# Second and first blocks of late operands: loaded by GpSimd's DMA queue in place of SyncE's

## The chip, the cores and the metric

The kernel runs on one core of one Trainium2 chip. The metric is the device time of one execution in microseconds (us), the median of several runs. The engines are named as in the profile: PE (TensorE), PEld (TensorE's weight loads), DVE (VectorE), ACT (ScalarE), POOL (GpSimd) and SP (SyncE, which here only issues DMAs). A "q" behind an engine's name means its sequencer, which waits and issues.

## The reference

One layer of a hybrid decoder, batch 1, 512 tokens, width 2048, all in float32:

```
h    = rmsnorm(x)
u, v, q, k, v_att, g_a, g_b = split(h @ w_in)              # 1024 columns each, the gates 2048
y_a  = gelu(u) * (tril(w_s) applied per chunk of 128 to rmsnorm(gelu(v)) + b_s)
y_b  = stick_breaking_attention(rmsnorm(q), rmsnorm(k), v_att)   # 8 heads, strictly causal
x   += (sigmoid(g_a) * (y_a @ w_up_a) + sigmoid(g_b) * (y_b @ w_up_b)) @ w_o
x   += (silu(gate) * up) @ w_ffn_out      where gate, up = split(rmsnorm(x) @ w_ffn_in)   # 5632 wide
x   += sigmoid(rmsnorm(x) @ w_ple_gate) * (p @ w_ple)
```

## The kernel before

Everything is held transposed: an operand is a row of blocks of 256 features by 512 tokens, each block 128 partitions by 1024 float32, or 512 KB. A product of two float32 numbers is made of three matmuls of parts (high by high, high by low, low by high): ACT rounds a value to its high part, DVE subtracts to get the low one. The tiles `whi` and `wlo` hold those parts of the weights, the arena `parts` those of the operand, and the arena `wholes` holds everything that is not yet split: weights as they land, blocks as they are loaded, results.

A block of weights by a block of the operand is either "plain" (kind P, four quarter products, lines 296 to 298) or "S" (seven products of sums of quarters in place of eight, line 692). S needs seven blocks of each side where P needs four, and the sums are made on the fly:

- **Weights** (class `Weights`). A weight unit of kind S has two landing loads on SP's queue (line 341: one quarter into two places; line 343: the other three quarters). Then POOL issues an accumulating DMA (`landed`, line 363) that adds two more quarters onto the doubled one. It can go only when line 341's load has landed. ACT then makes the high parts (line 359), DVE two more sums (line 375), and DVE the low parts (line 356). Four landing buffers and three slots of `whi`/`wlo` go round. A unit of kind P has one load on SP's queue (line 339) and no accumulating DMA.
- **Late operands** (`late_form` with `plain_first`). Where an operand of the next stage is only just finished, its block is first loaded and split as four plain quarters (lines 286, 287, or 541, 542 with a gain), and PE starts in kind P. The same block is then loaded a second time (`fetch_second`), DVE makes the sums of quarters (line 527, behind line 522 on ACT where there is a gain), they are split in their turn, and PE goes on in kind S. The first and the second load of such a block are the "first and second ones" of this change. Blocks of kind P (`plain_form`) have a first load alone.

The operands that go through HBM are `mix` (the merged branches, 8 blocks, for `w_o`), `x1` (8 blocks, for `w_ffn_in`), `hid` (22 blocks, for `w_ffn_out`, which is worked off in three passes of 8, 8 and 6 blocks) and `x2` (8 blocks, for the last gate). SP stores each block when it is made (lines 1344, 1386, 1405, 1442); `spilled_form` gives its loads. In the trace and in the order `x1` and `x2` are both `x`, and a load is line 518 whatever it reads. Other loads of line 518 are of `xT`, of the gates, of `ple` and, as residuals, of `x`.

The order of the work: PE's matmuls stand in program order; `tick()` puts between them, one step a time, what prepares the next stage (fetching a block, splitting it, fetching a second one). A scheduler then sets the order of each engine's instructions from the dependencies. On each engine, and on each DMA queue's issuing engine, instructions go in order: one that waits holds back those behind it. POOL's own work in these stages is the accumulating DMAs of weights, those of results into `x1` (line 1438), and one small power for each norm (line 974).

Of the kernel before, what the change touches and what calls it, by code (L numbers as in the profile page):

```python
# [70 lines left out]
def hybrid_layer(  # L71
# [18 lines left out]
    nc = tc.nc  # L90
# [9 lines left out]
    def nm(s):  # L100
        return f"{s}_{next(names)}"
# [14 lines left out]
    class Arena:  # L116
# [5 lines left out]
        def take(self, n, how="low"):  # L122


            spots = []
            for start, size in self.holes:
                end = start + size
                if how == "place":
                    start = -(-start // (2 * PLACE)) * 2 * PLACE
                if end - start >= n:  # L130
                    if how == "high":
                        spots.append((-end, end - n))
                    elif how != "old":
                        spots.append((start, start))
                    else:
                        spots.extend((self.given[a // P : -(-(a + n) // P)].max(), a)
                                     for a in {*range(start, end - n + 1, 256), end - n})
            at = min(spots)[1]
            start, size = next(h for h in self.holes if h[0] <= at < h[0] + h[1])
            self.holes.remove((start, size))  # L140
            self.holes.extend(
                h for h in ((start, at - start), (at + n, start + size - at - n)) if h[1])
            return Block(self, at, n)
# [369 lines left out]
    def cut(x):  # L513
        return x.rearrange("p (b c) -> p b c", c=256)

    def load(src, n=1024, how="old"):
        b = take(n, how)
        nc.sync.dma_start(out=b.f(0, 1024), in_=src)
        return b

    def gained(dst, src, gi, k):
# [770 lines left out]
    def y_form(c, i):  # L1292
        return plain_form((lambda: y_a[i]) if c == "a" else lambda: load(y_spill[i]),
                          lambda: len(y_done) == 8, raw=0 if c == "a" else 1024,
                          far=c == "b")
# [3 lines left out]
    for n, ((w, i), pr) in enumerate(zip(order, made())):  # L1299
# [25 lines left out]
        else:  # L1325
# [8 lines left out]
    spill = {(n, j): tc.dram_tile([P, 1024], F32, name=nm(n)) for n in ("mix", "x1", "x2")  # L1334
             for j in range(KU)}
    there = set()

    def spilled_form(kind, n, j, gain=None, **how):
        return (late_form if kind == "S" else plain_form)(
            lambda size=1024: load(spill[n, j], size), lambda: (n, j) in there, gain, far=True,  # L1340
            **how)

    def store(n, j, block):
        nc.sync.dma_start(out=spill[n, j], in_=block.f())
        there.add((n, j))
        give(block)

    ms = [spilled_form("S", "mix", j) for j in range(KU)]
    build(ms)
    for j in range(KU):  # L1350
        for b in "ba":
            s = load(gate_spill[b, j], 1024, "low")
            g = s.f()

            def gate(g=g):
                scaled(g, row1)
                nc.scalar.activation(g, g, AF.Sigmoid)

            after(1, gate)
            pr = pair([ys[b, i] for i in range(4)], last=j == KU - 1)  # L1360
            for h, ps in zip((g[:, :T], g[:, T:]), pr.ends()):
                nc.vector.tensor_tensor(out=h, in0=h, in1=ps, op=ALU.mult)
            if b == "b":
                part[j] = s
            else:
                nc.vector.tensor_tensor(out=g, in0=g, in1=part[j].f(), op=ALU.add)
                give(part.pop(j))
                after(1, lambda j=j, s=s: store("mix", j, s))
        if not j:
            ple_operands()  # L1370
        elif j < 6:
            ple_pair(j + 2)
            if j == 5:
                ple_done()
    give(norm1.block)


    norm2 = Norm()
    fs = [spilled_form("S", "x1", j, (g_ffn, j)) for j in range(KU)]
    for j in range(KU):  # L1380
        h = load(xT[j])
# [14 lines left out]
    for kinds in PASSES:  # L1396
        hs.append([spilled_form(k, "hid", u)
                   for u, k in enumerate(kinds, sum(map(len, hs)))])
# [25 lines left out]
    for c, units in enumerate(hs):  # L1424
# [3 lines left out]
        for j in range(KU):  # L1428
# [8 lines left out]
            if not end:  # L1437
                after(2, lambda o=o, j=j: nc.gpsimd.dma_start(
                    out=spill["x1", j], in_=o, accum_op=ALU.add))
# [134 lines left out]
```

## Time and profile before

| | |
|---|---|
| median of 3 runs | 2661.22 us (2660.4 to 2664.61) |
| profiled execution | 2659.74 us, of which its span, first to last instruction, 2658.0 us |
| granted TensorE clock | 0.999 |
| busy: PE, PEld, DVE, ACT, POOL | 99%, 87%, 84%, 53%, 17% |
| SP's DMA queue | 441.95 MB in 231136 packets, 50.7% of 16 DMA engines' span |
| POOL's DMA queue | 115.11 MB in 62112 packets, 27.5% |

The stages by time from the span's start: projections and branches to about 840 us, `w_up` to 1036, `w_o` to about 1160, `w_ffn_in` to about 2040, `w_ffn_out` in three passes to about 2190, 2345 and 2485, the gate to the end.

A row of a timeline reads: start, duration, engine, line, operation, what it writes and reads, count, and in brackets how long its engine was idle before it and what ended that. A row of waits reads: who waited for what, microseconds in total, times, the longest. A row of DMA issues ends with KB each and the median microseconds from issue to landing. A row of windows reads: the stretch, its length, busy microseconds and number of instructions of PE, PEld, DVE, ACT and POOL, granted clock, the DMA engines' busy share, GB/s.

### The profile page before, as it was taken

What the parts mean: (1) busy time and instruction counts of PE and PEld (TensorE: products, weight loads), DVE (VectorE), ACT (ScalarE), POOL (GpSimd) and SP (SyncE); (2) the same over time, 40 slices, a digit from 0 to 9 for tenths busy, and PEclk for the clock granted to TensorE, in tenths of its full rate; (3) what the DMA queues carried; (4) which work ended last, traced back from release to release, by engine and by line L of the source; (5) the groups of instructions that cost most, each with busy time, mean ns of one, the idle gap of its engine ahead of it and who ended that gap; (6) DMA issues with size and microseconds to landing.
All of it is one profiled execution on the core that took longest, in us unless ns stands there. A gap on an engine that the chain in (4) does not pass through costs nothing.

```text
span 2658.0 us, 42554 instructions
## 1 busy us (share of the span) xinstructions
PE 2638.2 (99%) x15336; PEld 2312.3 (87%) x15336; DVE 2234.6 (84%) x3821; ACT 1403.2 (53%) x2233; POOL 448.1 (17%) x556
## 2 busy tenths in 40 slices
PE   8999999999999999999999999999999999999999
PEld 7888888888998888888888888888888888889898
DVE  8687878787886558999888888888889989989876
ACT  7756565655554334566444444444445445455543
POOL 0122222232220001101111111111110211211110
PEclk9999999999999999999999999999999999999999
DMA  7677777777775668978888888788887989978884
GB/s 229 162 194 171 192 173 191 172 191 179 178 191 183 232 212 268 265 236 218 223 210 216 206 200 203 194 209 204 199 207 221 257 227 273 229 229 260 256 240 123
DMA packets 293459, 559.77 MB, mean 211 GB/s; under 512 B 26368, under 2 KB 140544, under 8 KB 293248
## 3 DMA queue, kind: packets, MB, share of 16 engines
q1 hardware_dynamic: 231136, 441.95, 50.7%
q0 software_dynamic: 62112, 115.11, 27.5%
q8 instruction: 120, 1.97, 0.3%
q14 instruction: 91, 0.75, 0.1%
HBM read 505.57 MB, written 51.38 MB: 210 GB/s over the span
## 4 chain that ended last, share of the span: by engine, by line
PE 90%; DVE 4%; DMA 3%; issue 1%; ACT 1%; SPq 0%; POOL 0%; ACTq 0%; POOLq 0%; DVEq 0%
PE ps L692 53%; PE ps L298 10%; PE ps L297 9%; PE ps L296 9%; PE small L692 6%; DVE wlo L356 1%; DVE wholes L527 1%; DMA wholes<-w_ffn_out 1%; PE small L1103 1%; PE small L1155 1%; DVE parts L287 1%; PE small L1029 1%; DMA x<-wholes 1%; ACT whi L359 0%; PE small L1214 0%
## 5 line engine op out<-in xcount | busy, mean ns | idle before, releaser
L692 PE MATMUL ps<-parts,whi 128*128 128x512 f32 x4200 | 1409.4, 398 | 1.6 <-DVE out L796 1.0
L359 ACT ACTIVATE whi<-wholes 128x512 fp32r<-128x512 f32 (+2 forms) x940 | 871.5, 941 | 745.8 <-DVE wholes L375 286.6
L356 DVE TENSOR_TENSOR wlo<-wholes,whi 128x512 fp32r<-128x512 f32 (+2 forms) x940 | 979.4, 1076 | 73.7 <-ACT whi L359 73.0
L692 PEld LDWEIGHTS ps<-parts,wlo 128*128 128x128 f32 x4200 | 790.2, 188 | 178.2 <-issue 1.9
L692 PE MATMUL ps<-parts,wlo 128*128 128x256 f32 x4200 | 831.3, 279 | 0.9 <-DVE wlo L356 0.9
L692 PEld LDWEIGHTS ps<-parts,whi 128*128 128x128 f32 x4200 | 677.1, 189 | 10.5 <-issue 3.6
L297 PE MATMUL ps<-parts,whi 128*128 128x256 f32 (+1 forms) x1832 | 605.0, 331 | 0.7 <-DVE parts L287 0.5
L298 PE MATMUL ps<-parts,wlo 128*128 128x256 f32 (+1 forms) x1832 | 604.9, 331 | 0.5 <-DVE wlo L356 0.5
L296 PE MATMUL ps<-parts,whi 128*128 128x256 f32 (+1 forms) x1816 | 597.3, 330 | 7.4 <-ACT parts L286 5.3
L297 PEld LDWEIGHTS ps<-parts,whi 128*128 128x128 f32 x1832 | 347.0, 189 | 39.0 <-DVE parts L287 2.7
L296 PEld LDWEIGHTS ps<-parts,whi 128*128 128x128 f32 x1816 | 343.6, 190 | 40.4 <-ACT parts L286 5.7
L298 PEld LDWEIGHTS ps<-parts,wlo 128*128 128x128 f32 x1832 | 347.3, 190 | 32.4 <-DVE wlo L356 1.6
L375 DVE TENSOR_TENSOR wholes<-wholes 128x256 f32<-128x256 f32 (+1 forms) x820 | 345.0, 421 | 17.9 <-DVE wlo L356 1.4
L751 DVE TENSOR_TENSOR out<-out,ps 128x256 f32<-128x256 f32 x490 | 202.3, 416 | 147.6 <-ACT out L748 147.4
L363 POOL DMA_DIRECT2D wholes<-w_ffn_in x169 | 147.1, 870 | 702.1 <-DVE wholes L375 251.7
L363 POOL DMA_DIRECT2D wholes<-w_in x132 | 116.6, 885 | 531.3 <-DVE wholes L375 132.8
L692 PE MATMUL small<-parts,whi 128*128 128x512 f32 x480 | 190.3, 397 | 0.0
L287 DVE TENSOR_TENSOR parts<-wholes,parts 128x1024 fp32r<-128x1024 f32 (+3 forms) x137 | 122.8, 907 | 18.5 <-ACT parts L286 18.5
L286 ACT ACTIVATE parts<-wholes 128x1024 fp32r<-128x1024 f32 (+3 forms) x137 | 106.5, 800 | 54.2 <-DVE wholes L527 35.7
L748 ACT ACTIVATE out<-ps 128x256 f32<-128x256 f32 x258 | 96.3, 383 | 50.7 <-PE ps L692 46.7
L363 POOL DMA_DIRECT2D wholes<-w_ffn_out x64 | 55.7, 871 | 360.6 <-DMA wholes<-w_ffn_out 89.2
L1402 ACT ACTIVATE out<-out 128x512 f32<-128x512 f32 x44 | 27.9, 633 | 155.6 <-DVE out L1401 155.6
(124 smaller groups left out, 1770.0 us busy)
## 6 DMA issues: line engine op xcount, KB each, us to landing
wholes<-w_ffn_in SPq DMA_DIRECT2D x169, 384.0 KB, 5.5
wholes<-w_in SPq DMA_DIRECT2D x132, 384.0 KB, 5.1
wholes<-w_ffn_in SPq DMA_DIRECT2D x169, 256.0 KB, 4.7
wholes<-w_ffn_in POOLq DMA_DIRECT2D x169, 256.0 KB, 5.3
wholes<-w_in SPq DMA_DIRECT2D x132, 256.0 KB, 4.3
wholes<-w_in POOLq DMA_DIRECT2D x132, 256.0 KB, 5.0
wholes<-w_ffn_out SPq DMA_DIRECT2D x64, 384.0 KB, 6.3
wholes<-x SPq DMA_DIRECT2D x45, 512.0 KB, 5.8
```

Of the source, the lines that this page charges most:

```text
L286: return (nc.scalar.activation(hi, src, AF.Copy), nc.vector.tensor_tensor(out=lo, in0=src, in1=hi.bitcast(F32), op=ALU.subtract))
L287: nc.vector.tensor_tensor(out=lo, in0=src, in1=hi.bitcast(F32), op=ALU.subtract))
L296: nc.tensor.matmul(ps, sh, mh, start=start, stop=False)
L297: nc.tensor.matmul(ps, sh, ml, start=False, stop=False)
L298: return nc.tensor.matmul(ps, sl, mh, start=False, stop=stop)
L356: in_turn(nc.vector.tensor_tensor(out=self.lo[:, blocks], in0=r, in1=h.bitcast(F32), op=ALU.subtract))
L359: in_turn(nc.scalar.activation(h, r, AF.Copy))
L363: nc.gpsimd.dma_start(out=raw[:, 3:5], in_=self.src[:, 1:3], accum_op=ALU.add)
L375: in_turn(nc.vector.tensor_tensor(out=o, in0=x, in1=y, op=ALU.add))
L692: m = nc.tensor.matmul(out, l, r, start=first and k == 0, stop=last and k == 1)
L748: in_turn(nc.scalar.activation(out, x, AF.Copy, scale=scale))
L751: in_turn(nc.vector.tensor_tensor(out=out, in0=x, in1=y, op=op))
```

## The change

The loads that `spilled_form` gives, first and second ones, go to GpSimd's queue. Nothing else is edited; the loads of `xT`, gates, `ple`, `y` and residuals stay on SP.

```diff
-    def load(src, n=1024, how="old"):
+    def load(src, n=1024, how="old", queue=nc.sync):
         b = take(n, how)
-        nc.sync.dma_start(out=b.f(0, 1024), in_=src)
+        queue.dma_start(out=b.f(0, 1024), in_=src)
         return b
...
     def spilled_form(kind, n, j, gain=None, **how):
         return (late_form if kind == "S" else plain_form)(
-            lambda size=1024: load(spill[n, j], size), lambda: (n, j) in there, gain, far=True,
+            lambda size=1024: load(spill[n, j], size, queue=nc.gpsimd), lambda: (n, j) in there, gain, far=True,
             **how)
```

What this does to the order shows at three places, each a piece of the difference (rows with "-" stand only in the order before, with "+" only in the order now; a number behind `mix`, `x` or `hid` tells blocks apart, and the lowest number is block 0).

SP's queue in the stage of `w_o`, where `mix` 8261 and 8262 are its last two blocks:

```order
-L518 DMA wholes<-mix_8261 128x1024
 L341 DMA wholes<-w_o 128x2x256
 L1386 DMA x_779_8263<-wholes 128x1024
 L343 DMA wholes<-w_o 128x768
-L518 DMA wholes<-mix_8262 128x1024
-L341 DMA wholes<-w_o 128x2x256
-L343 DMA wholes<-w_o 128x768
-L518 DMA wholes<-x_779_8263 128x1024
+L341 DMA wholes<-w_o 128x2x256
+L343 DMA wholes<-w_o 128x768
```

The three block loads are gone from between the loads of weights, which now follow each other.

POOL at the start of the first pass of `w_ffn_out`, where `hid` 10904 to 10911 are the pass's blocks:

```order
+L518 DMA wholes<-hid_10906 128x1024
+L363 DMA wholes<-w_ffn_out 128x512
+L518 DMA wholes<-hid_10907 128x1024
+L518 DMA wholes<-hid_10908 128x1024
+L363 DMA wholes<-w_ffn_out 128x512
+L518 DMA wholes<-hid_10909 128x1024
+L518 DMA wholes<-hid_10910 128x1024
+L363 DMA wholes<-w_ffn_out 128x512
 L1438 DMA x_779_8263<-out_18963 128x1024
```

The second loads now stand between the accumulating DMAs of the weights, one or two to a gap.

POOL at the start of the last pass, where `hid` 10923 is the last block of kind S that is loaded a second time, and `x` 787 and 788 are the first two blocks of `x2`:

```order
 L1438 DMA x_786_8270<-out_21604 128x1024
-L363 DMA wholes<-w_ffn_out 128x512 x11
+L363 DMA wholes<-w_ffn_out 128x512
+L518 DMA wholes<-hid_10923 128x1024
+L363 DMA wholes<-w_ffn_out 128x512
+L518 DMA wholes<-x_787_8271 128x1024
+L363 DMA wholes<-w_ffn_out 128x512
+L518 DMA wholes<-x_787_8271 128x1024
+L363 DMA wholes<-w_ffn_out 128x512
+L518 DMA wholes<-x_788_8272 128x1024
+L363 DMA wholes<-w_ffn_out 128x512
+L518 DMA wholes<-x_788_8272 128x1024
```

Eleven accumulating DMAs in a row became a row in which loads and accumulating DMAs take turns.

## The prediction

> **What bounds the kernel now.** First the page's row of busy time, then the stretches in which moved loads are issued (windows), then whom PE waited for from 820 us on.
>
> ```profile
> PE 2638.2 (99%) x15336; PEld 2312.3 (87%) x15336; DVE 2234.6 (84%) x3821; ACT 1403.2 (53%) x2233; POOL 448.1 (17%) x556
> ```
>
> ```profile
> 840.00:1030.00 190.00, 190.00 (x854) 158.01 (x853) 111.39 (x130) 69.96 (x79) 3.52 (x4) 1.00 0.67 223
> 1030.00:1060.00 30.00, 29.03 (x169) 25.17 (x168) 28.26 (x51) 16.84 (x22) 4.41 (x5) 1.00 0.93 281
> 1160.00:1220.00 60.00, 60.00 (x314) 51.35 (x313) 56.79 (x105) 45.13 (x68) 7.31 (x8) 1.00 0.82 238
> 1240.00:2020.00 780.00, 780.00 (x4476) 681.32 (x4476) 693.13 (x1244) 374.73 (x521) 137.46 (x158) 1.00 0.82 205
> 2030.00:2090.00 60.00, 60.00 (x329) 52.17 (x328) 59.51 (x98) 33.61 (x42) 8.77 (x10) 1.00 0.94 274
> 2190.00:2280.00 90.00, 88.47 (x485) 75.55 (x484) 85.36 (x143) 45.70 (x60) 15.50 (x18) 1.00 0.97 270
> 2360.00:2425.00 65.00, 64.54 (x388) 57.71 (x387) 57.46 (x93) 35.09 (x48) 7.54 (x9) 1.00 0.88 270
> sum 1760.00, PE 1756.95 PEld 1532.52 DVE 1511.52 ACT 856.01 POOL 256.97; mean PE 135.15 PEld 117.89 DVE 116.27 ACT 65.85 POOL 19.77
> ```
>
> ```profile
> PE ps L692 <- DVE out L796: 1.0, 2, 0.8
> PE ps L692 <- DVE wlo L356: 0.9, 1, 0.9
> ```
>
> PE is the bound. Over the 1760 us of the windows' answer (840 to 2630 without 1220 to 1240), which hold nearly all moved loads, it idles 1760.00 - 1756.95 = 3.05 us; its two largest waits there sum to 1.9. Before 840 no block is loaded from a spill, and the order there is as it was. So at most some 3.05 us can be gained, 0.11% of 2659.74. There is no such lid on a loss. The long stage of `w_ffn_in` (1240 to 2020) has DVE at 693.13 of 780 and slack; the seams between stages do not: in 2030:2090 DVE is busy 59.51 of 60 and the DMA engines 0.94. A delay of DVE in a seam has nowhere to go but PE, less whatever lead DVE had.
>
> **What is moved.**
>
> ```profile
> wholes<-x SPq DMA_DIRECT2D x45, 512.0 KB, 5.8
> wholes<-hid SPq DMA_DIRECT2D x42, 512.0 KB, 5.6
> wholes<-mix SPq DMA_DIRECT2D x16, 512.0 KB, 5.9
> x<-out POOLq DMA_DIRECT2D x16, 512.0 KB, 8.9
> wholes<-w_ffn_out POOLq DMA_DIRECT2D x64, 256.0 KB, 5.6
> ```
>
> Of the 45 loads of `x`, 16 are residuals (8 in the last pass, 8 in the gate) and stay; 29 + 42 + 16 = 87 loads go to POOL. They keep buffer, size and source, so the bytes are the same. POOL's own DMAs here all add, so no row prices a plain 512 KB load from POOL. Its bounds: a 256 KB adding one lands in 5.6 us, a 512 KB adding one in 8.9; against SP's 5.6 to 5.9 a load costs from -0.3 (5.6 - 5.9) to +3.3 (8.9 - 5.6). An adding packet reads both sides, so 256 KB of adding is the nearer work; I take +0.5.
>
> The Trainium skill, "DMA: Bandwidth & Descriptors", section Specifications, speaks against the change: first byte about 1 us on GpSimd's path, 0.6 on SyncE's. By it alone a load would cost +0.4, an estimate from that page; no row here shows the plain case.
>
> **Term 1, what SP gains.** SP's rows and PE's in the seam into `w_o`:
>
> ```profile
> 1030.85 0.54 SPq L343 DMA_DIRECT2D wholes<-w_o  x1
> 1037.37 0.33 SPq L518 DMA_DIRECT2D wholes<-mix  x1
> 1037.80 0.38 SPq L341 DMA_DIRECT2D wholes<-w_o  x1
> ```
>
> ```profile
> 1053.17 0.47 PE L692 MATMUL ps<-parts,whi 128*128 128x512 f32 x1 [0.80 <-DVE out L796]
> ```
>
> After its load of weights at 1030.85 SP stood before the block's load until 1037.37, and the weights at 1037.80 were held behind it. With the load on POOL these go up to 6 us earlier, unless their own landing buffer holds them. PE idles 0.97 us in 1030:1060. Bounds 0 and -3.05 (all idle time gone); I take -1.0. Elsewhere SP gains nothing that PE feels: what SP waits for longest is the landing buffers.
>
> ```profile
> SPq L341 <- DVE wlo L356: 1303.8, 376, 9.9
> SPq L518 <- DVE parts L287: 50.1, 30, 4.8
> ```
>
> These are 1303.8 us on buffers that DVE frees, and 50.1 on the loads' own largest wait, which moves to POOL with them.
>
> **Term 2, the seam at 2040 to 2080.** On POOL a load now stands behind accumulating DMAs, each of which waits until SP's load of its weights has landed. SP's loads of `hid` before, and POOL's DMAs at the same time:
>
> ```profile
> 2048.90 1.80 SPq L518 DMA_DIRECT2D wholes<-hid  x2
> 2055.72 0.33 SPq L518 DMA_DIRECT2D wholes<-hid  x1
> ```
>
> ```profile
> 2050.64 0.87 POOL L363 DMA_DIRECT2D wholes<-w_ffn_out  x1 [14.39 <-DVE parts L287]
> 2058.09 0.86 POOL L363 DMA_DIRECT2D wholes<-w_ffn_out  x1 [6.58 <-DVE wholes L527]
> ```
>
> `hid` 10907 was issued at 2048.90; now it stands behind the DMA that starts at 2050.64, so it goes at 2051.5 at the earliest, 2.6 late. 10909 (2055.72) goes after 2058.95, 3.2 late. DVE idles 0.49 us in all of 2030:2090, so before it had these blocks in time, and part of the delay is hidden. Bounds 0 and 3.2 (the delays overlap, they do not add); I take +1.0.
>
> **Term 3, the last pass.**
>
> ```profile
> 2369.43 0.33 SPq L518 DMA_DIRECT2D wholes<-hid  x1
> 2404.47 0.33 SPq L518 DMA_DIRECT2D wholes<-x  x1
> ```
>
> ```profile
> 2374.09 0.88 POOL L363 DMA_DIRECT2D wholes<-w_ffn_out  x1 [9.73 <-DMA wholes<-w_ffn_out]
> 2407.50 0.86 POOL L363 DMA_DIRECT2D wholes<-w_ffn_out  x1 [6.99 <-ACT parts L541]
> ```
>
> ```profile
> 2376.97 1.10 DVE L527 TENSOR_TENSOR wholes<-wholes 128x256 f32<-128x256 f32 x3 [2.46 <-DMA wholes<-hid]
> ```
>
> `hid` 10923 was issued at 2369.43, and DVE already idled 2.46 us for it. In the new order it stands behind the DMA of 2374.09, which ends at 2374.97: 5.5 us late, all of it DVE's. PE idles but 0.46 us in all of 2360:2425, so DVE had a lead, which no row measures. Bounds 0 and 5.5; I take +2.0, somewhat under half. The second load of `x` 788 (2404.47) stands behind the DMA of 2407.50: 3.9 late.
>
> ```profile
> 2390.01 1.34 ACT L541 ACTIVATE parts<-wholes,gcol 128x512 fp32r<-128x512 f32 x2 [2.77 <-DMA wholes<-x]
> 2405.99 1.34 ACT L541 ACTIVATE parts<-wholes,gcol 128x512 fp32r<-128x512 f32 x2 [4.80 <-DMA wholes<-x]
> 2409.07 1.34 ACT L522 ACTIVATE wholes<-wholes,gcol 128x512 f32<-128x512 f32 x2 [0.28 <-DMA wholes<-x]
> 2415.20 1.06 ACT L953 ACTIVATE out<-wholes 128x1024 f32<-128x1024 f32 x1 [3.63 <-DVE wholes L1441]
> ```
>
> ACT reads that second load at 2409.07 and some us later idles 3.63 for DVE, which covers nearly all of the 3.9. Bounds 0 and 3.9; I take 0.
>
> **Term 4, slower landing where someone already waits.** The rows above show three such loads (2.46, 2.77 and 4.80 us of waiting). Three times 0.5 is 1.5, and PE feels a part; bounds -0.9 (3 x -0.3) and 9.9 (3 x 3.3), taken +1.0.
>
> **Costed at nothing.** POOL's issuing time: 87 loads at some 0.87 us (the rows of line 363 above) make 76 us, covered by a POOL that is busy 256.97 of 1760 us. The loads of `hid` inside `w_ffn_in`, which wait on POOL for a store to land: should one hold an accumulating DMA, the weights' lead (landing buffers four deep) covers it, and the stage repeats without PE idling. The norm's power on POOL (line 974) now has one or two loads ahead of it, 1 to 2 us if nothing covers that:
>
> ```profile
> 2491.35 1.14 POOL L974 TENSOR_TENSOR cols<-mean,expo 128x4 f32<-128x4 f32 x1 [9.70 <-DVE mean L971]
> 2498.33 0.48 DVE L939 TENSOR_SCALAR diag<-ident,cols 128x128 f32<-128x128 f32 x2
> ```
>
> DVE takes its result 5.8 us after it is done (2498.33 - 2492.49).
>
> **Sum.** -1.0 + 1.0 + 2.0 + 1.0 = +3.0. The profiled execution took 2659.74, 1.48 less than the median of 2661.22, so 2662.7 there and 2664.2 as a median, +0.11%. A change under about 0.2% (5.3 us) can hardly be told from none; the three runs before lie 4.2 us apart.
>
> **The rivals.**
> - *POOL's order decides (slower), 0.32.* In the last pass the second load of `hid` behind an accumulating DMA costs PE its full 5.5, the 3.2 at 2050 comes through too, and `x` 788 brings 3.9: 5.5 + 3.2 + 3.9 = 12.6, less term 1: +11.6, 2672.8. It decides from the point where DVE's lead on PE at 2377 is under about 2 us. For it: DVE at 59.51 of 60, a DVE that already idled 2.46 for this load. Against: PE did not idle there.
> - *POOL's ring decides (slower), 0.10.* A 256 KB accumulating DMA that follows a 512 KB load on one queue lands later, by up to 3.3, in each of six seams (near 1010, 1180, 2050, 2200, 2240 and 2380); half of it felt in each gives 9.9, 2671. For it: DMA engines at 0.94 and 0.97. Against: POOL idles before each of these DMAs, so they start at once.
> - *Nothing is felt, 0.14.* All 16 DMA engines serve both queues; the loads land as before, and DVE's lead covers the order: 2661, with term 1 at 2660. The Trainium skill, "DMA: Bandwidth & Descriptors", section "Issuing engines are not separate DMA queues", says just this: DMAs from any engine run on the same DMA engines, and another issuer saves only time on its sequencer. The trace agrees in that SP's issue rows take 0.33 to 0.54 us.
> - *Faster, 0.06.* Weights on SP are never held by loads, and all idle time goes: 2661.2 - 3.05 = 2658.2. To be faster by over 0.2% it would need 5.3 us, more than PE idles, so that much gets 0.04 of the 0.06, for idle time that the rows may hide.
>
> That the loads don't move is ruled out by the order.
>
> **How the numbers follow.** My forecast has 0.38, from 2661 to 2667 (most of it under +5.3, a tenth of the whole above). Same: 0.28 of the forecast + 0.14 + 0.02 = 0.44, slower: 0.32 + 0.10 + 0.10 = 0.52, faster: 0.04. Slower thus has the most chance as a sign, though the likeliest single time is +3.0; the cases of slower spread up to the sum of the upper bounds, 3.2 + 5.5 + 3.9 + 9.9 = 22.5 (2683.7). The range leaves out its last part and the largest gain: 2659.5 to 2677.
>
> **What would show it.** Right: the first idle time of PE at 1050 shrinks; DVE's wait for `hid` near 2377 grows from 2.46 to 7 or 8 us; PE shows one or two new waits of 1 to 3 us in 2375 to 2420; POOL's load lands in 5.5 to 6.5. Wrong: PE's idle time in the seams sums to over 10 us (POOL's order), accumulating DMAs land well over 5.6 (the ring), or plain loads from POOL land in 8 and more, which would put term 4 at its upper end.

## The result, and the profile after

The changed kernel takes 2688.91 us (median of 5 runs, 2686.69 to 2693.53) against 2660.4 for the kernel before, run beside it (2656.82 to 2664.61): ratio 1.0112, 95% interval 1.0101 to 1.0124. That is +28.5 us, slower, and outside the predicted range of 2659.5 to 2677. The profiled execution took 2686.69, its span 2685.0 against 2658.0 before: 27.0 us to explain.

The page's row of busy time, after:

```profile
PE 2647.4 (99%) x15336; PEld 2316.0 (86%) x15336; DVE 2236.5 (83%) x3821; ACT 1404.4 (52%) x2233; POOL 497.8 (19%) x643
```

The same 15336 matmuls. PE's idle time is 2685.0 - 2647.4 = 37.6 us; before it was 2658.0 - 2638.2 = 19.8. So 17.8 us are new waits, and 9.2 (2647.4 - 2638.2) are matmuls that ran longer. The windows of after, at the seams as they lie there now:

```profile
1030.00:1060.00 30.00, 26.70 (x142) 22.83 (x141) 25.10 (x46) 15.15 (x20) 4.81 (x7) 0.91 0.89 254
1165.00:1225.00 60.00, 58.02 (x298) 48.80 (x297) 53.04 (x98) 44.17 (x66) 12.98 (x18) 1.00 0.82 232
1250.00:2030.00 780.00, 780.00 (x4475) 680.55 (x4474) 693.30 (x1244) 374.49 (x521) 140.20 (x163) 1.00 0.82 206
2040.00:2100.00 60.00, 56.63 (x300) 49.25 (x299) 55.08 (x92) 30.48 (x39) 13.61 (x20) 0.97 0.87 262
2205.00:2295.00 90.00, 86.51 (x471) 73.31 (x469) 82.29 (x137) 45.47 (x59) 22.71 (x32) 1.00 0.95 269
2375.00:2440.00 65.00, 61.45 (x340) 53.67 (x339) 50.22 (x78) 28.04 (x39) 9.45 (x13) 0.97 0.77 231
```

The long stage of `w_ffn_in` still runs without a gap; every seam has lost PE time, and in three the granted clock (the first number behind the brackets) is below 1. Whom PE waited for from 820 us on, where 1.0 was the largest before:

```profile
PE ps L297 <- DVE parts L287: 6.3, 5, 3.4
PE ps L692 <- DVE out L796: 4.2, 3, 2.8
PE ps L298 <- DVE wlo L356: 3.7, 5, 1.9
PE small L941 <- DVE diag L939: 2.4, 3, 1.1
PE ps L296 <- ACT parts L286: 1.9, 3, 1.1
```

POOL's DMA issues of after, with size and median time to landing:

```profile
wholes<-hid POOLq DMA_DIRECT2D x42, 512.0 KB, 6.8
wholes<-w_ffn_out POOLq DMA_DIRECT2D x64, 256.0 KB, 5.2
wholes<-x POOLq DMA_DIRECT2D x29, 512.0 KB, 6.1
wholes<-mix POOLq DMA_DIRECT2D x16, 512.0 KB, 7.7
```

The moved loads land in 6.57 us (median of all 87), 5.81 before. The accumulating DMAs land no later than before (5.2; 5.6 before). What does change is when the loads go. POOL's timeline in the first and in the last pass:

```profile
2059.24 0.88 POOL L363 DMA_DIRECT2D wholes<-w_ffn_out  x1 [6.03 <-DMA wholes<-w_ffn_out]
2059.84 1.35 POOL L518 DMA_DIRECT2D wholes<-hid  x2
...
2391.99 0.85 POOL L363 DMA_DIRECT2D wholes<-w_ffn_out  x1 [10.61 <-DMA wholes<-w_ffn_out]
2392.63 0.78 POOL L518 DMA_DIRECT2D wholes<-hid  x1
...
2431.48 0.86 POOL L363 DMA_DIRECT2D wholes<-w_ffn_out  x1 [6.07 <-ACT parts L541]
2432.04 0.86 POOL L518 DMA_DIRECT2D wholes<-x  x1
```

POOL stands 6 to 11 us in front of an accumulating DMA (line 363), and the load goes the moment after it. DVE and ACT then wait for the blocks:

```profile
2398.84 1.10 DVE L527 TENSOR_TENSOR wholes<-wholes 128x256 f32<-128x256 f32 x3 [8.22 <-DMA wholes<-hid]
2438.03 1.34 ACT L522 ACTIVATE wholes<-wholes,gcol 128x512 f32<-128x512 f32 x2 [5.21 <-DMA wholes<-x]
```

To place the loss I paired the n-th matmul of one trace with the n-th of another; the growth of PE's delay over a seam is what that seam cost. Times are those of before; runs are described below:

| | 1050 | 1184 | 2070 | 2220 | 2300 | 2390 | 2415 | 2510 |
|---|---|---|---|---|---|---|---|---|
| after | 5.2 | 4.1 | 4.8 | 1.3 | 1.9 | 4.4 | 3.6 | 2.0 |
| no accumulating DMAs, loads on POOL | 0.3 | 3.7 | 0 | 0.5 | -0.6 | 0 | -0.7 | 2.0 |
| seven loads back on SP | 3.1 | 5.1 | 1.4 | 2.0 | 0.1 | 0 | -0.1 | 1.0 |
| eleven loads back | 0.3 | 6.6 | 0 | 1.5 | 0.2 | 0 | -0.7 | 0.8 |
| loads ahead on POOL | 4.3 | 4.3 | 4.0 | 0.3 | 1.9 | 10.2 | 9.4 | -0.5 |

One profile has a few us of chance in it (a wait near 640, ahead of every moved load, costs some 3 us in some executions and is missing in others); single entries under about 1.5 say nothing. The profiled execution of the run with seven loads back is 5.6 us under that run's median. The same pairing gives how late each load was issued against PE's work (behind PE's own delay). For single loads lateness and landing are counted from the end of the issuing instruction; the medians count from its start.

| load | issued late, after | landing, before | landing, after |
|---|---|---|---|
| `mix` 8262, second | 1.4 | 4.7 | 6.0 |
| `hid` 10907, second | 2.4 | 3.2 | 5.2 |
| `hid` 10909, second | 1.8 | 4.6 | 5.8 |
| `hid` 10923, second | 6.7 | 7.2 | 5.4 |
| `x` 787, first and second | 4.3 and 7.5 | 3.6 and 5.1 | 6.7 and 7.7 |
| `x` 788, first and second | 2.6 and 5.7 | 4.5 and 4.3 | 4.6 and 5.1 |

So these blocks are late by their issue, and several by their landing too.

### The profile page after: what moved, and what is told of

Its sections match the earlier page's. It is cut to its first block, busy times and chain, and to the rows that moved or that the text cites. A ratio compares the mean times of both kernels' runs of the same rounds, so it can differ in the third digit from the quotient of the medians.

```text
span 2685.0 us, 42569 instructions
## 1 busy us (share of the span) xinstructions
PE 2647.4 (99%) x15336; PEld 2316.0 (86%) x15336; DVE 2236.5 (83%) x3821; ACT 1404.4 (52%) x2233; POOL 497.8 (19%) x643
## 4 chain that ended last, share of the span: by engine, by line
PE 86%; DVE 5%; DMA 4%; ACT 2%; issue 2%; POOL 0%; POOLq 0%; SPq 0%; ACTq 0%; DVEq 0%
PE ps L692 52%; PE ps L298 9%; PE ps L297 9%; PE ps L296 9%; PE small L692 6%; DVE wlo L356 2%; DMA wholes<-x 1%; DMA wholes<-w_ffn_out 1%; DVE parts L287 1%; DVE wholes L527 1%; DVE out L751 1%; DMA wholes<-hid 1%; PE small L1155 1%; PE small L1103 1%; PE small L1029 1%
## 5 line engine op out<-in xcount | busy, mean ns | idle before, releaser
L692 PEld LDWEIGHTS small<-parts,wlo 128*128 128x128 f32 x480 | 90.4, 188 | 18.7
```

The lines of the kernel that those rows point to most:

```text
L692: m = nc.tensor.matmul(out, l, r, start=first and k == 0, stop=last and k == 1)
```

## Experiments

The theory drawn from this profile is that POOL's order decides: a load is late because of what stands ahead of it. The rivals: POOL's ring and slower landing (the queue itself, wherever a load stands in it), company (the accumulating DMAs that run beside the loads on that queue, whatever the order), the spread of the edit over first and second loads, and the scheduler's new order on other engines.

**Half of the change at a time.** Only second loads on POOL, then only first ones:

```diff
-            lambda size=1024: load(spill[n, j], size, queue=nc.gpsimd), lambda: (n, j) in there, gain, far=True,
+            lambda size=1024: load(spill[n, j], size, queue=nc.sync if size == 1024 else nc.gpsimd), lambda: (n, j) in there, gain, far=True,
```

> Only the second loads go to GpSimd's queue, the first ones stay on SP's. The changed kernel is 28.5 us slower; by its trace PE falls behind at some eleven places, and at all but three (the first loads of x 786, 787 and 788) the block that is late is a second one. Order (a load stands behind accumulating DMAs that wait for their weights to land): nearly all of it, +19 to +25, about 2682. Path (a plain load from GpSimd's queue lands later wherever it stands): the same places, but shared with the first loads by number waited for: +15 to +20. Clock (a wait of PE of some 2.7 us or more is followed by 4 to 6 us at half the granted clock): 2 to 4 windows with a clock of about 0.5, as in the changed kernel.

> Only the first loads go to GpSimd's queue. Order: the first loads of w_o, w_ffn_in and the first two passes have 8 to 100 us to spare and cost nothing; those of x 787 and 788 in the last pass and of x 786 are late: +3 to +7, about 2665. Path: +2 to +4. Were the loss something spread (POOL busy issuing, the weights' accumulating DMAs held back everywhere), half of it would be here: +14.

Seconds 2686.43 (1.0108, 1.0093 to 1.0123), firsts 2675.77 (1.0064, 1.0049 to 1.0079), before 2658.92. 27.5 and 16.9 make more than 28.5: the halves do not add up. The first loads alone lost over twice the +3 to +7 that order was to cost, and more than the +14 named for something spread. But it is not spread: `w_ffn_in` lost nothing, and by the pairing 9.9 of it fall on the two seams with a norm (5.5 at 1184, 4.4 at 2510), where PE waits 3.54 and 3.12 us for the diagonals (line 939). So the loss doesn't belong to one kind of load.

**Without the accumulating DMAs.** Line 363 becomes `pass`, in the kernel before and in the changed one; weights then lack two added quarters.

> The kernel before without the accumulating DMAs of the weights (their quarters are not added, so the products of those sums are left out of the result). POOL then issues only the DMAs of results into x1 in these stages. It is the footing for the next run. PE's instructions are the same, so all theories expect the kernel before less its few waits: 2655 to 2661.

> The changed kernel without the accumulating DMAs of the weights (same part of the computation left out): the loads stand alone on GpSimd's queue. Order: they are issued as early as on SP's, and the difference to the run without accumulating DMAs and with loads on SP falls from 28.5 to under 5. Path (landing 0.4 to 0.9 us later at eleven waited places, and the clock on top): 8 to 15 stay. Ring (a load behind a load on GpSimd's queue starts late because the ring of descriptors is full): 10 or more stay, with loads in pairs landing 8 us and more after issue.

2654.01 (0.9985, 0.9975 to 0.9994) with SP's queue, 2659.72 (1.0006, 0.9996 to 1.0015) with POOL's. The price of POOL's queue falls from 28.5 to 5.7 us (under 5 was expected from order), and the seams at 1050, 2070, 2390 and 2415 are gone. Landing of `hid`, with SP's queue and with POOL's:

```profile
wholes<-hid SPq DMA_DIRECT2D x42, 512.0 KB, 5.0
```

```profile
wholes<-hid POOLq DMA_DIRECT2D x42, 512.0 KB, 5.0
```

Over all 87 loads the medians are 5.20 and 5.19. So a plain load from POOL lands no slower by itself. This removes the company as well as the order; the next runs try to part them.

**The ring.** A larger scratch for POOL's descriptors (1024 to 1536 bytes a partition, paid for by one buffer of `diag` in place of two):

```diff
-                   dynamic_dma_scratch_size=1024)
+                   dynamic_dma_scratch_size=1536)
```

> The changed kernel with half as much room again for the descriptors of GpSimd's queue (1536 in place of 1024 bytes a partition; the memory comes from one of two buffers of the norms' diagonal). Order and company of the accumulating DMAs: nothing changes, 2685 to 2693. Ring (loads and accumulating DMAs wait for room for descriptors): much of the 28.5 us comes back, 2665 to 2675, and the median landing of loads from GpSimd's queue falls from 6.6 to under 6.

2687.22 (1.0112, 1.0094 to 1.0131): nothing changes, and all seams stay. With the 5.2 us of the accumulating DMAs this theory falls.

**Another in-order queue.** `queue=nc.scalar` in place of `nc.gpsimd`:

> The same loads on ScalarE's queue: off SP's queue as in the changed kernel, but with no accumulating DMA ahead of them; they stand behind ScalarE's own work. Order and company: the loads land in 5.5 to 6 us again, and what is lost is only what ScalarE's waits cost: 2660 to 2672. Sharing (two queues divide the DMA engines, so an urgent load no longer goes ahead of the weights that SP issues behind it): the loads land in 6.3 to 7 us, and 10 us or more of the loss stay whichever second queue it is: 2670 to 2688.

2676.76 (1.0069, 1.0054 to 1.0084). The loads land in 5.86 us, as from SP, and yet 17.3 us are lost. ACT's timeline shows one of the places:

```profile
1037.17 0.33 ACTq L518 DMA_DIRECT2D wholes<-mix  x1
1037.54 1.09 ACT L715 ACTIVATE out<-ps 128x512 f32<-128x512 f32 x2 [6.47 <-DMA x<-wholes]
```

ACT stood 6.47 us in front of a load, for the store that it waits for, with its own work behind it. Against PE's work this load went out 2.5 us late and landed 1.4 sooner, and the engine paid; `hid` 10907 went out 4.5 late. So another in-order queue, without accumulating DMAs, loses too.

**How long a wait PE feels, and what it costs then.** In the kernel before, DVE repeats one split of weights (line 356) 2 to 14 times at nine places in `w_ffn_in`, where no load is late:

```diff
-                    split(True, slice(5, 7), s)
+                    for _ in range(1 + late.get(self.unit, 0)): split(True, slice(5, 7), s)
```

> The kernel before, with DVE held up at nine units of weights of w_ffn_in, some 70 us apart, by 2, 3, 4, 5, 6, 7, 8, 10 and 14 repeats of one subtraction of 0.6 us: waits of PE of about 1, 1.5, 2, 2.7, 3.3, 4, 4.5, 5.7 and 8 us, 33 us in all. Clock: behind each wait of 2.7 us and over, PE runs 4 to 6 us at half its granted clock and loses 2 to 3 us more; behind the waits under 2 it loses nothing more: 2659 + 33 + 13 = 2705. No clock effect: 2659 + 33 = 2692, with the matmuls' spacing the same behind the waits.

2669.99 (1.0045, 1.0028 to 1.0061). Up to 8 repeats (some 5 us) nearly vanish in DVE's lead, so most of the expected waits did not come; 10 and 14 reach PE:

```profile
PE small L692 <- DVE wlo L356: 3.6, 1, 3.6
PE ps L692 <- DVE wlo L356: 2.4, 1, 2.4
```

Windows around the wait of 2.4, then around that of 3.6:

```profile
1804.00:1806.00 2.00, 0.06 (x1) 0.06 (x1) 1.93 (x4) 0.00 (x0) 0.00 (x0) 1.00 0.78 107
1806.00:1808.00 2.00, 2.00 (x12) 1.78 (x13) 1.97 (x6) 0.00 (x0) 0.00 (x0) 1.00 0.14 25
...
1884.00:1886.00 2.00, 1.66 (x6) 1.39 (x6) 1.97 (x6) 1.88 (x3) 0.00 (x0) 0.50 0.00 0
1886.00:1888.00 2.00, 2.00 (x10) 1.75 (x9) 2.00 (x4) 0.18 (x1) 0.00 (x0) 0.75 0.01 2
```

The clock stays at 1.00 behind the first and is halved behind the second, which cost about 2.2 us more after its 3.8 (a wait of 0.34 is in it). The changed kernel has the same behind its wait at 1050 (PE's row, then windows):

```profile
1052.82 0.50 PE L692 MATMUL ps<-parts,whi 128*128 128x512 f32 x1 [2.76 <-DVE out L796]
```

```profile
1056.00:1058.00 2.00, 2.00 (x8) 1.73 (x7) 1.84 (x4) 0.79 (x1) 0.00 (x0) 0.50 0.75 136
1058.00:1060.00 2.00, 2.00 (x8) 1.71 (x8) 1.48 (x2) 1.95 (x3) 0.00 (x0) 0.50 0.84 217
```

**Earlier issue.** A higher priority for the load in the scheduler:

```diff
-        queue.dma_start(out=b.f(0, 1024), in_=src)
+        with tc.high_priority(400 if queue is nc.gpsimd else 0): queue.dma_start(out=b.f(0, 1024), in_=src)
```

> The changed kernel with the loads first in the order of GpSimd's queue where both could go: x 784, hid 10918 and x 787's second load come ahead of the accumulating DMA that they stood behind, and x 781 and the last two of x2 ahead of the norm's power; hid 10907 and 10923 and mix 8262 stay. Order: x 787's second load was 3.8 us late and comes 2 to 4 earlier, so 2 to 5 us of the loss come back: 2684 to 2687. Company alone (landing beside accumulating DMAs, whatever the order): nothing, 2686 to 2692.

2683.55 (1.0094, 1.0079 to 1.0109): 4.4 us less, with intervals that overlap, and not where I expected. The second load of `x` 787 went right behind the first, 3.8 late by the measure above (7.5 in the changed kernel), as its block's store had come late; that of 788 stayed behind its accumulating DMA:

```profile
2423.71 0.85 POOL L363 DMA_DIRECT2D wholes<-w_ffn_out  x1 [6.12 <-ACT whi L359]
2424.33 0.79 POOL L518 DMA_DIRECT2D wholes<-x  x1
```

The seams at 2390 and 2415 did not improve (3.9 and 6.2), so the run decides little.

**Some loads back on SP.** Seven of 87 (the second of `hid` 10907, 10909 and 10923, both of `x` 787 and 788); then four more (the second of `mix` 8261 and 8262, the first of block 7 of `x1` and of `x2`):

```diff
+BACK = {("hid", 3, 1280), ("hid", 5, 1280), ("hid", 19, 1280), ("x2", 0, 1024), ("x2", 0, 1280), ("x2", 1, 1024), ("x2", 1, 1280)}
...
+            lambda size=1024: load(spill[n, j], size, queue=nc.sync if (n, j, size) in BACK else nc.gpsimd), lambda: (n, j) in there, gain, far=True,
```

> The changed kernel with seven loads back on SP's queue: those that stand on GpSimd's queue right behind an accumulating DMA that waits for its weights (hid 10907, 10909 and 10923, second loads) and the first and second ones of x 787 and 788; the other 80 stay. In the changed kernel PE falls behind by 4.8 us at 2030 to 2110 and by 8.0 at 2383 to 2430 of the kernel before's time. Order: these two come back, all but about 2, so -10 to -12, to about 2678, and the other four seams keep their 12 to 14 us. Something spread (80 loads beside the accumulating DMAs, POOL's time, bandwidth): under 5 come back, 2684 and over.

> As the run before, and also the second loads of mix 8261 and 8262 and the first ones of x 786 and 794 back on SP's queue; 76 loads stay on GpSimd's. Order: the seam at 1050 (5.2 us in the changed kernel) comes back too, and part of those at 1184 (4.1) and 2498 (2.0): 2664 to 2670, most of the 28.5. What would stay is what the scheduler did to DVE's order at 1184 (next run) and the waits at 2216 and 2278. Something spread: 2678 and over.

2674.69 (1.0059, 1.004 to 1.0078) and 2669.44 (1.0044, 1.003 to 1.0058): 8% of the loads bring back 13 of 28.5 us, 13% of them 18. The seam at 1184, which was to shrink with eleven back, grew to 6.6. With seven back the seams at 2070, 2390 and 2415 give back 11.5 of 12.8 us, and DVE's wait for `hid` 10923 is 2.87, near its 2.46 of before:

```profile
2385.90 1.09 DVE L527 TENSOR_TENSOR wholes<-wholes 128x256 f32<-128x256 f32 x3 [2.87 <-DMA wholes<-hid]
```

**A trial that missed.** All loads on SP again, each behind a one-column memset of its block on POOL, which was to bring POOL's order without its queue:

> All 87 loads go out on SP's queue, but each waits for a small memset that POOL makes in the block at about the load's place in POOL's order (the load overwrites it): POOL's order without GpSimd's queue. The memsets stand at the same places or one accumulating DMA earlier or later, and SP holds its weights while it waits. Order: most of the loss is here though no load runs on GpSimd's queue: 2675 to 2695, with loads landing in 5.5 to 6. Company on the queue (loads slow beside accumulating DMAs on one queue): under 2668.

2661.39 (1.0007, 0.9998 to 1.0016). The memsets did not stand where the loads do in the changed kernel but earlier, so the loads were at most 0.1 us late at the places above. It shows that loads in time cost nothing, and doesn't part order from company.

**Order against company, on the same queue.** All 87 loads on POOL; the seven above are ordered ahead of the one or two accumulating DMAs they stood behind:

```diff
+AHEAD_OF, adding = {("hid", 3, 1280): 1, ("hid", 5, 1280): 1, ("hid", 19, 1280): 1, ("x2", 0, 1024): 2, ("x2", 0, 1280): 2, ("x2", 1, 1024): 2, ("x2", 1, 1280): 2}, []
```

> The changed kernel, all 87 loads still on GpSimd's queue; only the order of that queue differs at seven of them: the second of hid 10907, 10909 and 10923 stands ahead of the one accumulating DMA (L363) that it stood behind, and those of x 787 and 788 ahead of up to two. The order theory expects most of the delay of the PE in the two seams near 2070 and 2400 to go (of 4.8 and 8.0 us in the changed kernel) and the total to fall by about 6 to 11 us, to 2678-2683; the seams near 1050, 1184, 2220 and 2300 keep theirs. The rival, that company on GpSimd's queue makes the loads late wherever they stand, expects the two seams unchanged and the total at 2687-2690.

2694.81 (1.0128, 1.011 to 1.0146): slower still, as neither theory said. The loads of `hid` are in time: by the measure above 10907, 10909 and 10923 are at most 0.6 us late (2.4, 1.8 and 6.7 in the changed kernel). Those of `x` are nearer to it: the second of 787 is 1.6 late and that of 788 2.6, the first ones are early. So company alone doesn't make loads go late. Their landing is 3.1 to 7.0 us. Now the accumulating DMAs stand behind loads that wait for stores; POOL, then DVE and PE:

```profile
2400.70 0.54 POOL L518 DMA_DIRECT2D wholes<-x  x1 [15.08 <-DMA x<-wholes]
2401.36 1.77 POOL L363 DMA_DIRECT2D wholes<-w_ffn_out  x2
```

```profile
2391.14 1.10 DVE L527 TENSOR_TENSOR wholes<-wholes 128x256 f32<-128x256 f32 x3 [2.24 <-DMA wholes<-hid]
2408.00 0.89 DVE L375 TENSOR_TENSOR wholes<-wholes 128x256 f32<-128x256 f32 x2 [9.60 <-DMA wholes<-w_ffn_out]
```

```profile
2409.33 0.58 PE L296 MATMUL ps<-parts,whi 128*128 128x256 f32 x1 [6.28 <-ACT whi L359]
```

DVE's wait for `hid` is back at 2.24, but it waits 9.60 us for weights, and PE 6.28, then 2.98 near 2432, and 2.41 in the seam at 2070. Both kinds of DMA wait for something late, and on one queue one always holds the other. My expectation missed that the swap only chooses which.

**The seam at 1184**, which no term named. The scheduler changed two orders there. On DVE the last split of the last block of `x1` (line 542, `x` 786) now stands ahead of the norm's diagonals (line 939); on ACT the rounding of that block (line 541) and the next second block's gain (line 522) stand ahead of one rounding of weights (line 359). DVE's order alone, first made in the kernel before:

```diff
+            if t == 0 and split_last[0]: tc.add_manual_dep(i.ins, split_last[0], mybir.DependencyInfo(mybir.DependencyClass.NoSync, mybir.DependencyReason.DATA), reason="behind the split")
```

> The kernel before, all loads on SP, with one constraint on the order: DVE makes the first diagonal of the norm (line 939) behind the split of the last first load of x (line 542), where the scheduler puts it in the changed kernel too. Scheduler's order: PE waits for the diagonal at 1184 and falls behind by 1 to 4 us there and nowhere else: 2660 to 2663. The load alone: no difference, 2657 to 2661, and the 4.1 us at 1184 in the changed kernel are the loads' alone. The times will hardly tell 2 us; the trace does.

2657.7 (0.9996, 0.9987 to 1.0005), the seam -0.2. Then DVE's old order put back in the changed kernel, and in the one with eleven loads back:

> The changed kernel with the norm's order on VectorE near 1184 put back as in the kernel before: the last two halves of the last block of x (L542) stand behind the four diagonals (L939) and no longer ahead of them. If the scheduler's order there is what cost the 4.1 us in this seam, they go and the total falls by about 4, to 2685; if late loads of x cost it, the seam stays within 1.5 us of its 4.1 and the total at 2689. The other seams stay.

> Eleven of the 87 loads on SP's queue as in the earlier run, and the norm's order on VectorE near 1184 as in the kernel before. If order and late loads together make the seam (6.6 us in that run), and the loads of x 787 back on SP have ended the lateness, the seam goes and the total comes to about 2662-2664. If the order has no part, it stays at 2669.

2688.13 (1.0099, 1.0077 to 1.0121) and 2671.62 (1.0043, 1.0028 to 1.0058): the seam keeps 4.6 and 7.6 us, so DVE's order is not the cause. ACT's row for the first load of `x` 786, before, and in the last run with PE's wait behind it:

```profile
1184.20 1.32 ACT L541 ACTIVATE parts<-wholes,gcol 128x512 fp32r<-128x512 f32 x2
```

```profile
1182.85 1.33 ACT L541 ACTIVATE parts<-wholes,gcol 128x512 fp32r<-128x512 f32 x2 [4.03 <-DMA wholes<-x]
```

```profile
1186.16 0.80 PE L941 MATMUL small<-diag,ones 128*128 128x128 f32 x2 [3.17 <-DVE diag L939]
```

ACT did not wait for that load before; here it waits 4.03 us, with weights behind it that it used to round first. So ACT's old order was put back: in the changed kernel, with eleven loads back, and without the accumulating DMAs.

```diff
+    chain, highs, gained_highs, seconds_gained, ordered = {}, [], [], [], []; behind = lambda: len(highs) >= 393 and len(gained_highs) >= 16 and len(seconds_gained) >= 20 and not ordered and ordered.extend([tc.add_manual_dep(a.ins, highs[392].ins.name, mybir.DependencyInfo(mybir.DependencyClass.NoSync, mybir.DependencyReason.DATA), reason="behind the weights") for a in gained_highs[14:16] + seconds_gained[18:20]])
```

> The changed kernel with ACT's order near 1184 put back as in the kernel before: the split of the last block of x (L541) and the gain of the next second block (L522) stand behind one more rounding of weights (L359) and not ahead of it; DVE's order then comes back by itself. If ACT's order is what costs PE the 4.1 us in this seam, its loss falls to under 1.5 and the total by some 3 to 5, to about 2685; if late loads cost it, it stays at 4 to 5. The other seams stay.

> Eleven of the 87 loads on SP's queue, and ACT's order near 1184 as in the kernel before. The order theory expects the seam (6.6 and 7.6 us in the runs with eleven) under 1.5 and the total at 2661 to 2665; the theory of late loads expects 6 to 8 and 2669 to 2672.

> All 87 loads on POOL's queue, the accumulating DMAs of all weights left out (weights lack two added quarters), and ACT's order near 1184 as in the kernel before. The seam there cost 3.7 us in this kernel without the last edit. The order theory expects it under 1 and the total at 2655 to 2657, within 3 us of the same kernel on SP's queue (2654.01 earlier); late loads expect 2659 to 2660.

2685.52 (1.0101, 1.0084 to 1.0118), 2668.57 (1.0034, 1.0023 to 1.0045) and 2658.94 (1.0002, 0.9993 to 1.0011), between the two expectations; the totals alone don't separate from the same kernels without this edit. In the seam the cost falls from 4.1 to 2.1, from 6.6 to 4.4 and from 3.7 to 1.5: some 2.1 each time, so ACT's order likely makes about 2 us. It is not shown for certain, with one profile each: the run with the higher priority has the changed kernel's order on ACT and DVE in this seam and costs 2.0 there. The rest stays with the loads: with eleven back ACT still waits 3.18 for `x` 786, which is then issued by SP, 1.0 late, and lands in 7.8 us where it took 5.1 before. In that run it goes out 0.3 us behind another load of `x` on POOL's queue, and that one takes 7.7. Before and in the changed kernel the two go on one queue, and `x` 786 lands in 5.1 and 3.2. That two loads at once on two queues slow each other would fit; no run tests it alone.

## Why the prediction was wrong, point by point

The path was foreseen, its price was not. What failed is the step that lets a lead of DVE, which no row measured, swallow most of each load's delay (terms 2 and 3, and `x` 788 at 0), and the gain of term 1. The runs show the delays reaching PE: 5.2, 4.8, 4.4 and 3.6 us in the four seams where -1.0, +1.0, +2.0 and 0 stood, and 9.3 more in seams without a term.

- **What bounds the kernel**: right. PE lost in the seams alone, and `w_ffn_in` lost nothing. (The 1760 us of the windows leave out 2020 to 2030 too, beside 1220 to 1240.)
- **The price of a plain load from POOL, +0.5**: about right; +0.8 in the median, and 0 where nothing accumulates beside it, so the +0.4 that stands beside it in the prediction does not show (5.19 against 5.20).
- **Term 1, SP's gain of 1.0**: wrong in sign, +5.2 in that seam. The weights did go earlier (line 341 at 1035.02; 1037.80 before) and nobody needed them. DVE already waited 1.17 us for the second load of `mix` 8262, a row that the term leaves out; issued 1.4 later and landing in 6.0 for 4.7, it made DVE wait 3.69 and PE 2.76, and a second wait of 0.54 and the halved clock added the rest. DVE's rows before and after:

```profile
1042.51 1.10 DVE L527 TENSOR_TENSOR wholes<-wholes 128x256 f32<-128x256 f32 x3 [1.17 <-DMA wholes<-mix]
```

```profile
1044.85 1.10 DVE L527 TENSOR_TENSOR wholes<-wholes 128x256 f32<-128x256 f32 x3 [3.69 <-DMA wholes<-mix]
```

- **Term 2, +1.0**: 4.8. The delays forecast, 2.6 and 3.2, were 2.4 and 1.8 in fact, and the two blocks landed 2.0 and 1.2 us slower on top; PE waited 3.37 and the clock fell. Taking a third, on the strength of a lead that no row measured, was the error.
- **Term 3, +2.0**: mechanism and place right (DVE's wait grew from 2.46 to 8.22, "7 or 8" was forecast), size wrong: 4.4. The step that failed outright is `x` 788 at 0: its second load was 5.7 late, not 3.9, and those of `x` 787, which I costed nowhere, 4.3 and 7.5; the seam took 3.6. I had counted one accumulating DMA's wait, but each late load puts off those behind it: the first load of `x` 787 stood 11.30 us for its own block's store, which came late.
- **Term 4, +1.0**: what PE felt of it is not separable from the others. The landing of its three loads changed by -1.8, +3.1 and +0.1; that the sum, 1.4, is near three times 0.5 is luck.
- **Costed at nothing**: POOL's issuing time and the loads inside `w_ffn_in` were rightly free. The norm's seam at 2510 shows 2.0, but 3.6 in the run on SP's queue without accumulating DMAs (there in the slowest of ten executions), so that is not laid to the change. The seam at 1184, 4.1, was missing from the list, and with it that the scheduler moves instructions of ACT and DVE, which the order showed and I did not price.
- **The half clock**: no term had it. It held for 13.65 us behind new waits (6.83, 3.41 and 3.41), over which PE's delay grew by some 5.0 us beyond its waits; the other 4.2 of the 9.2 us of longer matmuls are not placed. Without the 5.0 the median would have been some 2684, still above the range. The upper bounds summed to 22.5: the seams that they cover came to 18.0, and the seams not summed (1184, 2220, 2300, 2510) add 9.3.
- **The rivals**: "POOL's order decides" (0.32) is the one that came true, by its own sign: PE's new idle time is 17.8 us, over 10. Its +11.6 us is the part that was thought of, three places, and under half of what came. "POOL's ring" fell by its own run, "nothing is felt" and "faster" by the total.

The cause of most of the loss is shown from three sides: with the accumulating DMAs gone (5.7 left of 28.5), with seven loads on SP (13 back) and with the loads' place alone changed (those of `hid` in time, at the weights' cost). Open are how the 4.1 us at 1184 divide, and the share of the slower landing: at 1050 and 2070 it is about as large as the later issue (1.3 beside 1.4 for `mix` 8262, 2.0 beside 2.4 for `hid` 10907), in the last pass smaller.

The rule that I cited of the Trainium skill, "DMA: Bandwidth & Descriptors", section "Issuing engines are not separate DMA queues", holds for the transfer (5.20 and 5.19 us). Its saving on the issuing sequencer alone does not cover this case: with accumulating DMAs in front of the loads and beside them on that queue the change cost 28.5 us, without them 5.7.

## What to carry to other kernels

A DMA queue is chosen by what its issuing engine waits for, not by how busy it is: POOL was busy 17% and still the wrong place, since its DMAs wait up to 11 us for another engine's loads. Before a load is moved, list for each place what stands ahead of it, what that waits for, and how long its reader already waits; where the reader has no idle row of slack, count the whole delay. Where PE idles some 1.4 us or more within 3.41 us, half clock may follow (next section); each 3.41 us of it cost some 1.5 us here.

## What was not expected of the hardware

The granted clock halves behind short waits of PE, and the length of the wait alone does not decide. A wait of 2.40 us left it at 1.00 (above); one of 2.41 us, in the run with the loads ahead, did not:

```profile
2071.53 1.01 PE L296 MATMUL ps<-parts,whi 128*128 128x256 f32 x3 [2.41 <-ACT parts L286]
```

The clock records of the traces settle it. Half clock comes in pieces of 3.41 us, or of two or three times that, and within one execution all of them begin and end on one grid with steps of 3.41 us. The two steps that the wait of 2.40 us touches, then the step with the wait of 2.41 and the one behind it:

```profile
1801.66:1805.07 3.41, 1.88 (x10) 1.23 (x8) 3.27 (x5) 0.00 (x0) 0.86 (x1) 1.00 0.40 88
1805.07:1808.48 3.41, 2.54 (x15) 2.27 (x16) 3.34 (x9) 0.00 (x0) 0.00 (x0) 1.00 0.31 54
...
2068.11:2071.52 3.41, 1.01 (x9) 0.80 (x7) 3.41 (x6) 1.84 (x2) 0.88 (x1) 1.00 0.90 293
2071.52:2074.93 3.41, 3.40 (x14) 3.21 (x15) 3.41 (x7) 1.06 (x1) 2.14 (x3) 0.50 0.90 188
```

The first wait lies across the end of a step and leaves PE idle for 1.53 us in one and 0.87 in the next; the second lies in one step, idle for 2.40. In the 20 traces, from 830 us to shortly before the end, 37 steps at full clock were followed by half clock: all 31 in which PE idled 1.8 us or more, 6 of the 21 with 1.43 to 1.8, none with less. Once there, the half clock went on for a second step with as little as 0.54 us of idle time (the changed kernel, from 1054.30). Its third stretch, from 2409.39, follows waits of 0.23 and 1.36 us in one step, so a row of short waits will do.

The Trainium skill, "TensorE: Matmul & The Clock Gate", Part 1, tells of half speed after an idle window of about 3.4 us that runs freely, so that the point varies; these traces agree on the length and on its running freely, but here 1.43 us of idle time in such a window could be enough.
